# Ends of the last two layers worked by halves of the tokens: one half projected while the other goes through residual and norms

## The chip, the cores and the metric

The kernel runs on one core of a Trainium2 chip. The core has five engines with a queue of instructions each: TensorE (PE in the profile; PEld is its weight load) multiplies matrices, VectorE (DVE), ScalarE (ACT) and GpSimd (POOL) work element by element, SyncE (SP) issues the DMAs. An engine takes the instructions of its queue in order and waits at each until what it needs is there. The metric is the time of one launch on the device in microseconds; the median of three runs before the change is 2830.22 us (2822.88, 2830.22 and 2830.51).

## The reference, cut to what matters

Two blocks of two layers each work on x, 512 tokens of 1024 features, in float32. The last layer of the second block is the one that matters here (`l` is 1, `need_ctx` false):

```python
y, yc = mixer_odd(h, hc, rows, cols, od_w_in[o], od_qk_norm[o], od_lambda[o], od_subln[o],
                  od_w_out[o], diff_lambda_init(l), need_ctx)      # ends in concat(oc, od) @ w_out
x = x + g1 * rms_norm_2(y, norm_g[l, 1])
h = rms_norm_2(x, norm_g[l, 2]) * (1.0 + sc2) + sh2
x = x + g2 * rms_norm_2(swiglu(h, ffn_w_in[l], ffn_w_out[l]), norm_g[l, 3])

def swiglu(h, w_in, w_out):
    g, u = jnp.split(h @ w_in, 2, axis=-1)
    return (jax.nn.silu(g) * u) @ w_out                            # hidden width 2816
```

There are two ends: the mixer's output projection, then residual, norm and the norm ahead of the feed-forward part; and the second feed-forward projection, then norm, residual and the output. Every norm needs the sum of squares over all 1024 features of a token; tokens are independent of each other.

## The kernel before, in words

Activations lie with features on the 128 partitions: x is a tile of 128 x 8 x 512 (feature within a block, block `k`, token). A float32 product is made of three matmuls on halves of the mantissa: `hi` and `lo` of the weights (`wh`, `wl`) with `hi` and `lo` of the activations (`hh`, `hl`; `hid` for the hidden layer). `dense` makes one unit, 128 output features for all tokens, from one call of `weights`: SP loads `wr` (three buffers, L417), ScalarE casts it to `wh` (L422), and POOL subtracts to get `wl` (L398), except that every third unit's goes to VectorE (L400); `wh` and `wl` have two buffers each. A buffer `wr` is free once `wl` is made.

A projection (`out_proj`, and the last loop of `ffn`) runs over eight units `f`. For each, `proj` adds the matmul's result into y (VectorE, L625), squares it (ScalarE, L503) and sums the squares (POOL, L631). Units go in turn to the PSUM tags `d` and `b`, two buffers each.

`boundary` then works all 512 tokens at once. `rstd` sums the squares over partitions by small matmuls against a column of ones, scales them (VectorE, L481), takes the power -1/2 (POOL, L483) and spreads the result by transposing matmuls (L498). `postnorm_tile` makes the residual in eight tiles, a product on VectorE (L576) and a sum (L577) by turns on POOL and VectorE. `prenorm_steps` squares x, sums in seven VectorE additions (L515, L518), calls `rstd` again, and `norm_tile` makes `hh` and `hl` tile by tile (L554 to L560). Where `early` holds weights, `outer` then runs the first four units of the feed-forward part, with the loop over `k` outside, so that it can start with the first norm tile; `prepare` loads and splits those four weights (`u0` to `u3`) during the projection.

The mixer's output projection runs in two parts: inputs 0 to 3 are projected earlier (`out_head`), and the part in question has inputs 4 to 7, so its weights are 128 x 512 and a unit has 12 matmuls. The feed-forward part works its 22 hidden blocks in groups of 8, 8 and 6, each group projected and added into y; the last one has units of 128 x 768 and 18 matmuls.

The order of the work on each engine is set by a scheduler that takes the recorded instructions by their priority. `weave` interleaves streams of steps by rate: (stream, rate, offset of priority).

Of the kernel before, what the change touches and what calls it, by code (L numbers as in the profile page):

```python
# [11 lines left out]
F32 = mybir.dt.float32  # L12
F32R = mybir.dt.float32r
# [10 lines left out]
KD = D // 128  # L24
S = 512
# [174 lines left out]
class Net:  # L200
# [136 lines left out]
    def first(self, g, n):  # L337
        for _ in range(n):
            next(g)
            yield  # L340
# [196 lines left out]
            except StopIteration as e:  # L537
                return e.value

    def prenorm_steps(self, x, T, gain, shift, pool=None, al=None):  # L540
# [4 lines left out]
        h = self.new_h(T, pool)  # L545
        for k in range(n):
            self.norm_tile(h, x, k, T, r, gain, shift, al)
            yield
        return h
# [56 lines left out]
            yield  # L606
            return h, dict(enumerate(acc))

    def outer(self, ws, h, acc, ks=range(KD)):

        for k in ks:
            w = slice(k * 128, k * 128 + 128)
            for (hi, lo), a in zip(ws, acc):
                self.mm(a, hi[:, w], h[0][:, k, :], k == 0, False)
                self.mm(a, hi[:, w], h[1][:, k, :], False, False)
                self.mm(a, lo[:, w], h[0][:, k, :], False, k == KD - 1)

    def proj(self, f, ps, y, sq, T, first=True, last=True):

# [1111 lines left out]

        return self.lagged((block(h) for h in range(4)), -50)

    def ffn(self, l, h, T, hid_new, ready={}):
        nc, I = self.nc, self.I
        wi, wo = I["ffn_w_in"], I["ffn_w_out"]
        y, sq = self.oy(T), None
        for gi, (j0, n) in enumerate(HGROUPS):
            hid = hid_new()
            for j in range(n):  # L1740
                pg, pu = (ready.pop(2 * (j0 + j) + i) if ready else
                          self.dense(wi[l, i * NFH + j0 + j].rearrange("p k c -> p (k c)"), h, T, tag="db"[i])
                          for i in range(2))
                g = self.silu2(pg, T)
                nc.vector.scalar_tensor_tensor(g, g, 0.5, pu, op0=ALU.mult, op1=ALU.mult)  # L1745
                self.split(g, hid[0][:, j, :], hid[1][:, j, :], 1.0, "dve" if j in ([0, 2, 4, 6], [7])[l] else "pool")
                yield
            for f in range(KD):
# [21 lines left out]
    def run(self):  # L1770
# [125 lines left out]
        with self.phase("early") as ph:  # L1896
            early = []

            def prepare():
                for u in range(4):  # L1900
                    src = I["ffn_w_in"][1, u % 2 * NFH + u // 2].rearrange("p k c -> p (k c)")
                    early.append(self.weights(src, 1024, (ph, f"u{u}")))
                    yield

            y, sq = self.weave((self.out_proj(I["od_w_out"], h, S, y, range(4)), 8, 0),
                               (prepare(), 4.2, 0))
            h, ready = self.weave((self.boundary(y, sq, x4, m(1), m(2), x1, early), 1, 0))
            self.close_y()
            self.stage(low=3)
            with self.phase("ffn") as ph:  # L1910
                hid = lambda: [self.tl(ph, [128, KD, S], F32R, "hid", 2) for _ in range(2)]
                y, sq = self.result(self.ffn(1, h, S, hid, ready))
        self.result(self.boundary(y, sq, x1, m(3), None, self.out))

# [66 lines left out]
```

## Time and profile before

| | us |
|---|---|
| runs, median of three | 2830.22 |
| the profiled execution, its own time | 2819.89 |
| its span, first to last instruction | 2818.1 |
| TensorE busy | 2455.0 (87%) |
| VectorE, ScalarE, POOL busy | 1258.7, 1188.2, 1079.4 (45%, 42%, 38%) |

The profiled execution is 10.3 us below the median of the runs. Times in rows are microseconds from the start of its span, so the span ends at 2818.1. In a row of the timeline the bracket at the end is how long the engine was idle before, and what ended the wait. TensorE's matmuls are pipelined: a row's duration overlaps the next one, so the pace is read from the starts.

### The profile page before, as it was taken

To read this page: it belongs to the slowest core of one execution; us is meant where nothing else is said; L and a number is where in the kernel's file an instruction comes from. 1 tells how busy PE (TensorE), PEld (TensorE's weight loads), DVE (VectorE), ACT (ScalarE), POOL (GpSimd) and SP (SyncE) were. 2 spreads that over 40 slices of the span, in tenths; PEclk is the share of its full clock that TensorE was granted. 3 is DMA by queue.
4 is the path that set the end of the run, shared out by engine and by line. 5 is a ranking of instruction groups with operands and counts; after the bars stand their busy time and mean duration, and the time that the engine had idled before them with its cause. 6 is when DMAs were issued, how large, how long until landed. Compare 5 with 4: busy or idle time off the path is not lost. (4 is left out here: it accounts for less than half of the span.)

```text
span 2818.1 us, 35394 instructions
## 1 busy us (share of the span) xinstructions
PE 2455.0 (87%) x13052; PEld 1994.9 (71%) x13052; DVE 1258.7 (45%) x2065; ACT 1188.2 (42%) x2227; POOL 1079.4 (38%) x754
## 2 busy tenths in 40 slices
PE   6988896778888886769999899999888989799997
PEld 4765666666666665648998777777776777688886
DVE  3655357235646644445442631212645767421212
ACT  3534365333547534445554522222434646332222
POOL 2435235344533551213455732322542222443334
PEclk9988998888979987879999999999988989899998
DMA  7364644344344652335553545454444253333332
GB/s 244 121 205 156 207 165 154 107 140 162 104 124 139 213 182 100 116 112 143 174 159 135 186 135 172 149 169 133 148 140 158 90 153 113 113 100 97 94 97 75
DMA packets 170816, 400.56 MB, mean 142 GB/s; under 512 B 19378, under 2 KB 60820, under 8 KB 167316
## 3 DMA queue, kind: packets, MB, share of 16 engines
q1 hardware_dynamic: 170644, 398.31, 43.7%
q8 instruction: 103, 1.69, 0.2%
q14 instruction: 69, 0.57, 0.1%
HBM read 339.85 MB, written 58.39 MB: 141 GB/s over the span
## 5 line engine op out<-in xcount | busy, mean ns | idle before, releaser
L398 POOL TENSOR_TENSOR wl<-wr,wh 128x1024 fp32r<-128x1024 f32 (+3 forms) x245 | 538.2, 2198 | 899.5 <-ACT wh L422 451.5
L422 ACT CAST wh<-wr 128x1024 fp32r<-128x1024 f32 (+3 forms) x367 | 353.8, 964 | 706.5 <-PE d L389 279.5
L389 PE MATMUL d<-hh,wh 128*128 128x512 f32 x960 | 398.4, 415 | 19.7 <-ACT hh L556 7.8
L389 PE MATMUL d<-hl,wh 128*128 128x512 f32 x960 | 394.0, 410 | 1.9 <-DVE hl L557 0.9
L389 PE MATMUL d<-hh,wl 128*128 128x512 f32 x960 | 263.5, 403 | 0.0
L400 DVE SCALAR_TENSOR_TENSOR wl<-wr,wh 128x1024 fp32r<-128x1024 f32 (+3 forms) x122 | 152.1, 1246 | 227.8 <-PE d L389 91.9
L389 PEld LDWEIGHTS d<-hh,wh 128*128 128x128 f32 x960 | 190.6, 199 | 62.2 <-ACT hh L556 8.4
L389 PEld LDWEIGHTS d<-hl,wh 128*128 128x128 f32 x960 | 189.7, 198 | 42.5 <-issue 2.5
L389 PEld LDWEIGHTS d<-hh,wl 128*128 128x128 f32 x960 | 185.0, 195 | 39.6 <-issue 1.6
L400 DVE SCALAR_TENSOR_TENSOR pg<-b,pg 128x512 fp32r<-128x512 f32 (+1 forms) x208 | 137.2, 665 | 68.7 <-ACT pg L404 67.2
L389 PE MATMUL b<-hh,wh 128*128 128x512 f32 x416 | 164.2, 395 | 0.0
L389 PE MATMUL b<-hl,wh 128*128 128x512 f32 x416 | 163.2, 392 | 0.0
L934 POOL TENSOR_TENSOR oy<-pg,pg 64x256 f32<-64x256 f32 (+1 forms) x72 | 57.7, 802 | 262.3 <-DVE pg L932 91.3
L404 ACT CAST pg<-b 128x512 fp32r<-128x512 f32 (+1 forms) x208 | 117.1, 570 | 80.2 <-PE b L909 68.2
L882 DVE TENSOR_REDUCE sm<-s 128x1 f32<-128x768 f32 (+3 forms) x144 | 120.7, 846 | 26.6 <-PE s L389 25.9
L389 PE MATMUL d<-hc,wh 128*128 128x256 f32 x656 | 105.4, 311 | 23.7 <-DVE rp L400 11.8
L950 DVE SCALAR_TENSOR_TENSOR rp<-rp,d 128x512 f32<-128x512 f32 (+1 forms) x77 | 46.7, 607 | 165.5 <-ACT rp L949 165.4
L1745 DVE SCALAR_TENSOR_TENSOR rp<-rp,b 128x512 f32<-128x512 f32 (+1 forms) x64 | 38.1, 595 | 175.3 <-PE b L389 174.8
L389 PE MATMUL d<-hid,wh 128*128 128x512 f32 (+1 forms) x528 | 114.7, 361 | 1.5 <-POOL hid L398 1.5
L389 PEld LDWEIGHTS d<-hc,wh 128*128 128x128 f32 x656 | 94.9, 211 | 28.3 <-ACT wh L422 12.2
L389 PE MATMUL b<-hid,wh 128*128 128x512 f32 (+1 forms) x528 | 110.8, 361 | 0.0
L389 PE MATMUL b<-hh,wl 128*128 128x512 f32 x416 | 103.8, 389 | 0.0
(416 smaller groups left out, 5143.2 us busy)
## 6 DMA issues: line engine op xcount, KB each, us to landing
wr<-in_ffn_w_in SPq DMA_DIRECT2D x132, 512.0 KB
mr<-in_ada_w SPq DMA_DIRECT2D x96, 512.0 KB
wr<-in_ffn_w_out SPq DMA_DIRECT2D x48, 512.0 KB
x<-x SPq DMA_DIRECT2D x20, 1024.0 KB
wr<-in_w_in SPq DMA_DIRECT2D x38, 512.0 KB
mr<-in_w_mod SPq DMA_DIRECT2D x32, 512.0 KB
wr<-in_ev_w_in SPq DMA_DIRECT2D x20, 512.0 KB
wr<-in_ffn_w_out SPq DMA_DIRECT2D x24, 384.0 KB
```

The costliest lines, as they stand in the source:

```text
L389: self.nc.tensor.matmul(out, lhsT, rhs, start=start, stop=stop)
L398: self.nc.gpsimd.tensor_sub(out, src, hi)
L400: self.nc.vector.scalar_tensor_tensor(out, src, scale, hi, op0=ALU.mult, op1=ALU.subtract)
L404: self.nc.scalar.copy(hi, src)
L422: nc.scalar.copy(hi[:, :n], raw[:, :n])
L882: nc.vector.reduce_max(c, s, axis=AX.X, negate=True)
L934: nc.gpsimd.tensor_tensor(d, sel(t), sel(rs), op=ALU.mult)
L950: nc.vector.scalar_tensor_tensor(t, t, 1.0, ps, op0=ALU.add, op1=ALU.mult)
L1745: nc.vector.scalar_tensor_tensor(g, g, 0.5, pu, op0=ALU.mult, op1=ALU.mult)
```

## The change

`ending` takes the place of `out_proj` with `boundary` at the last layer's first end, and of the last group's loop with `boundary` at its second. `proj_half` projects the eight units for one half of the tokens (256 columns), loading and splitting each unit's weights for each half. First half 0 is projected, with `prepare` beside it; then half 1, woven with `norm(0)`: residual, store of x and norm of half 0. Then `norm(1)` is woven with `first(0)`, the early matmuls of half 0, and `first(1)` follows. At the second end there is no early part, and `norm(1)` comes last. `prenorm_steps` can write into a given tile, `outer` can start and stop a sum at other places, and `ffn` can return ahead of its last projection. Tiles `bp` for the residual are ten of half the width, not eight of the full one.

```diff
+    def proj_half(self, c, wsrc, h, y, ks):
+
+        cols, sq = self.half(c), None
+        hv, yv = [t[:, :, cols] for t in h], [t[:, :, cols] for t in y]
+        for f in range(KD):
+            ps = self.dense(wsrc(f), hv, S // 2, ks, "db"[f % 2])
+            sq = self.proj(f, ps, yv, sq, S // 2, False)
+            yield
+        return sq
+
+    def ending(self, proj, y, xsrc, gain, nxt, xdst, early=(), beside=None):
...
+            al = partial(self.tl, ph, dt=F32, tag="bp", bufs=10), self.bank
+            h = self.new_h(S) if nxt is not None else None
+            acc = []
+
+            def norm(c, sq):
+                cols = self.half(c)
+                xv = x[:, :, cols]
+                yield from self.postnorm_steps(xv, [t[:, :, cols] for t in y], sq, S // 2, gain, al)
+                for i in range(2):
+                    nc.sync.dma_start(xdst[:, 4 * i:4 * i + 4, cols], xv[:, 4 * i:4 * i + 4])
+                if nxt is not None:
+                    yield from self.prenorm_steps(xv, S // 2, *nxt, al=al, into=[t[:, :, cols] for t in h])
+
+            def first(c):
+                cols = self.half(c)
+                for k in range(KD):
+                    self.outer(early, [t[:, :, cols] for t in h], [a[:, cols] for a in acc], [k], c == 0, c == 1)
+                    yield
+
+            sq = self.weave(*[(proj(0), 8, 0)] + [(beside, 8, 0)] * (beside is not None))
+            sq = self.weave((proj(1), 8, 0), (norm(0, sq), 17, 0))
+            if not early:
+                self.steps(norm(1, sq))
+                return h
...
+            self.weave((norm(1, sq), 17, 0), (first(0), 8, -150))
+            self.steps(first(1))
+            return h, dict(enumerate(acc))
...
-            y, sq = self.weave((self.out_proj(I["od_w_out"], h, S, y, range(4)), 8, 0),
-                               (prepare(), 4.2, 0))
-            h, ready = self.weave((self.boundary(y, sq, x4, m(1), m(2), x1, early), 1, 0))
...
+            wsrc = lambda f: I["od_w_out"][f, :, 4:8].rearrange("p k c -> p (k c)")
+            ho, yo = h, y
+            h, ready = self.ending(lambda c: self.proj_half(c, wsrc, ho, yo, range(4, 8)), y, x4, m(1), m(2), x1, early,
+                                   prepare())
...
+            f = self.ffn(1, h, S, hid, ready, True)
...
+            self.ending(lambda c: self.proj_half(c, wsrc, hidden, y, range(n)), y, x1, m(3), None, self.out)
```

On POOL, at the first end. Before, from a late unit's low part to the power of the sums (`sm_20985`); `wl` is a unit's low part, `rp` the sum of squares:

```order
L398 TENSOR_TENSOR wl_20893<-wr_20890,wh_20892 128x512
L631 TENSOR_TENSOR rp_20778<-rp_20778,rp_20858 128x512
L398 TENSOR_TENSOR wl_20922<-wr_20919,wh_20921 128x512
L631 TENSOR_TENSOR rp_20778<-rp_20778,rp_20887 128x512
L398 TENSOR_TENSOR wl_20945<-wr_20942,wh_20944 128x512
L631 TENSOR_TENSOR rp_20778<-rp_20778,rp_20910 128x512
L631 TENSOR_TENSOR rp_20778<-rp_20778,rp_20939 128x512
L398 TENSOR_TENSOR wl_21247<-wr_21244,wh_21246 128x1024
L483 TENSOR_TENSOR sm_20985<-sm_20983,mhalf 128x4
```

Now, from the fourth early weight's low part (`u3l`) to the power for half 0 (`sm_21005`):

```order
L398 TENSOR_TENSOR u3l_20882<-wr_20879,u3h_20881 128x1024
L398 TENSOR_TENSOR wl_20888<-wr_20885,wh_20887 128x512
L686 TENSOR_TENSOR rp_20790<-rp_20790,rp_20905 128x256
L398 TENSOR_TENSOR wl_20934<-wr_20931,wh_20933 128x512
L686 TENSOR_TENSOR rp_20790<-rp_20790,rp_20928 128x256
L398 TENSOR_TENSOR wl_20957<-wr_20954,wh_20956 128x512
L686 TENSOR_TENSOR rp_20790<-rp_20790,rp_20951 128x256
L398 TENSOR_TENSOR wl_21022<-wr_21019,wh_21021 128x512
L398 TENSOR_TENSOR wl_21051<-wr_21048,wh_21050 128x512
L483 TENSOR_TENSOR sm_21005<-sm_21003,mhalf 128x2
```

An early weight's low part has come to POOL, ahead of half 0's fifth unit (`wl_20888`), and two low parts of half 1 (`wl_21022`, `wl_21051`) stand ahead of half 0's power.

On TensorE, at the second power of half 0 at the first end (`b_21128` takes its ones-matmuls, `b_21135` its transposes, `b_21180` is unit 5 of half 1, `d_21212` unit 6):

```order
L389 MATMUL b_21128<-blk,bp_21105 128x1 x2
L389 MATMUL d_21212<-hh_19715,wh_21208 128x256
L389 MATMUL d_21212<-hl_19716,wh_21208 128x256
L389 MATMUL d_21212<-hh_19715,wh_21208 128x256
L389 MATMUL d_21212<-hl_19716,wh_21208 128x256
L389 MATMUL d_21212<-hh_19715,wl_21209 128x256 x2
L498 MATMUL b_21135<-ident,sm_21133 128x128 x2
L389 MATMUL b_21180<-hh_19715,wh_21176 128x256
```

Before, nothing was left to project there:

```order
L389 MATMUL b_20974<-blk,rp_20778 128x1 x4
L389 MATMUL b_20974<-blk,rp_20962 128x1 x4
L498 MATMUL b_20987<-ident,sm_20985 128x128 x4
L389 MATMUL b_21041<-blk,bp_21018 128x1 x4
L498 MATMUL b_21050<-ident,sm_21048 128x128 x4
L389 MATMUL d_21093<-hh_21055,u0h_20782 128x512
```

Units 5 and 7 of half 1 have moved behind the transposes of half 0's second norm.

On SP, at the end of the program, before:

```order
L417 DMA wr_23204<-in_ffn_w_out 128x768 [waits DMAHW0_49,DVE_49]
L417 DMA wr_23233<-in_ffn_w_out 128x768 [waits DMAHW1_49,Pool_49]
L417 DMA wr_23262<-in_ffn_w_out 128x768 [waits DMAHW2_49,Pool_49]
L417 DMA wr_23291<-in_ffn_w_out 128x768 [waits DMAHW3_49,DVE_49]
L593 DMA out<-x_23326 128x2048 [waits DVE_49,Pool_49] x2
```

Now:

```order
L417 DMA wr_23885<-in_ffn_w_out 128x768 [waits DMAHW3_49,Pool_49]
L649 DMA out<-x_23470 128x4x256 [waits DVE_49,Pool_49]
L417 DMA wr_23914<-in_ffn_w_out 128x768 [waits DMAHW5_49,Activation_49,Pool_49]
L649 DMA out<-x_23470 128x4x256 [waits DVE_49,Pool_49]
L417 DMA wr_23943<-in_ffn_w_out 128x768 [waits DMAHW4_49]
L649 DMA out<-x_23470 128x4x256 [waits DVE_49,Pool_49] x2
```

The two stores of half 0 stand ahead of the loads of the last two units of half 1.

## Rows read from the trace of the kernel before

**Rows 1.** Busy time by stretches; columns: stretch, length, busy (count) per engine, clock, DMA.
```profile
2393.40:2413.30 19.90, 18.96 (x84) 15.34 (x83) 10.03 (x11) 11.41 (x18) 16.86 (x13) 1.00 0.55 166
2413.30:2436.20 22.90, 5.90 (x33) 4.97 (x33) 14.37 (x24) 5.84 (x11) 10.44 (x7) 0.58 0.37 138
2436.20:2460.90 24.70, 24.70 (x97) 19.72 (x98) 8.77 (x12) 7.71 (x12) 5.21 (x4) 0.91 0.00 1
2766.30:2799.80 33.50, 33.24 (x145) 26.97 (x144) 8.13 (x11) 10.06 (x14) 16.34 (x11) 1.00 0.16 47
2799.80:2818.10 18.30, 3.14 (x21) 2.54 (x19) 8.99 (x14) 0.63 (x1) 7.23 (x5) 0.57 0.28 115
```

**Rows 2.** Timeline, first end; columns: start, us, engine, line, operation, out<-in, count, idle before.
```profile
2413.18 2.35 POOL L398 TENSOR_TENSOR wl<-wr,wh 128x1024 fp32r<-128x1024 f32 x1
...
2415.50 1.02 POOL L483 TENSOR_TENSOR sm<-sm,mhalf 128x4 f32<-128x4 f32 x1
...
2417.60 2.06 DVE L576 SCALAR_TENSOR_TENSOR bp<-oy,x,b 128x512 f32<-128x512 f32 x3 [2.17 <-PE b L498]
...
2424.79 0.98 DVE L577 TENSOR_TENSOR x<-x,bp 128x512 f32<-128x512 f32 x1
...
2429.42 0.69 DVE L518 TENSOR_TENSOR bp<-bp,bp 128x512 f32<-128x512 f32 x1
...
2436.16 0.79 PE L389 MATMUL d<-hh,u0h 128*128 128x512 f32 x1 [1.60 <-ACT hh L556]
```

**Rows 3.** Timeline of TensorE, 256-column matmuls of the context's feed-forward part.
```profile
1564.16 1.98 PE L389 MATMUL b<-hc,wh 128*128 128x256 f32 x16
1565.97 1.07 PE L389 MATMUL b<-hc,wl 128*128 128x256 f32 x8
```

**Rows 4.** Timeline, the first end's projection: POOL, ScalarE, VectorE and the loads.
```profile
2395.29 2.55 POOL L398 TENSOR_TENSOR wl<-wr,wh 128x512 fp32r<-128x512 f32 x2 [5.86 <-PE b L389]
...
2396.61 0.80 SPq L417 DMA_DIRECT2D wr<-in_od_w_out  x2
...
2397.79 1.29 POOL L631 TENSOR_TENSOR rp<-rp,rp 128x512 f32<-128x512 f32 x1
...
2397.86 0.33 SPq L417 DMA_DIRECT2D wr<-in_ffn_w_in  x1
...
2399.28 0.62 ACT L422 CAST wh<-wr 128x512 fp32r<-128x512 f32 x1 [1.86 <-DMA wr<-in_od_w_out]
...
2402.15 1.05 ACT L422 CAST u3h<-wr 128x1024 fp32r<-128x1024 f32 x1 [0.89 <-DMA wr<-in_ffn_w_in]
...
2403.24 1.62 DVE L400 SCALAR_TENSOR_TENSOR u3l<-wr,u3h 128x1024 fp32r<-128x1024 f32 x1 [1.05 <-ACT u3h L422]
...
2403.88 2.13 POOL L631 TENSOR_TENSOR rp<-rp,rp 128x512 f32<-128x512 f32 x1
```

**Rows 5.** Groups by line and shape, whole run; busy and mean ns of one, then idle before.
```profile
L398 POOL TENSOR_TENSOR wl<-wr,wh 128x768 fp32r<-128x768 f32 x26 | 49.6, 1907 | 48.1 <-ACT wh L422 26.3 <-PE d L389 14.4 <-issue 5.1
L625 DVE TENSOR_TENSOR oc<-d,oc 128x256 f32<-128x256 f32 x8 | 3.4, 423 | 7.2 <-PE d L389 7.1
L503 ACT ACTIVATE rp<-oc 128x256 f32<-128x256 f32 x16 | 6.6, 414 | 3.3 <-DVE oc L625 2.9
```

**Rows 6.** Timeline of POOL, a sum of squares of 256 columns, undisturbed.
```profile
1596.25 0.74 POOL L631 TENSOR_TENSOR rp<-rp,rp 128x256 f32<-128x256 f32 x1
```

**Rows 7.** Timeline, the second end.
```profile
2798.45 1.53 PE L389 MATMUL b<-hid,wl 128*128 128x512 f32 x6
2799.83 0.94 PE L389 MATMUL s<-blk,rp 128*128 128x1 f32 x8
...
2804.99 2.07 DVE L576 SCALAR_TENSOR_TENSOR bp<-oy,x,s 128x512 f32<-128x512 f32 x3 [2.31 <-PE s L498]
...
2809.65 3.94 SPq L593 DMA_DIRECT2D out<-x  x2
...
2812.18 0.98 DVE L577 TENSOR_TENSOR x<-x,bp 128x512 f32<-128x512 f32 x1
```

More of the change, by code (lines that the diff above doesn't have):

```diff
@@ L538, in run_through, with prenorm_steps @@
                 return e.value
-    def prenorm_steps(self, x, T, gain, shift, pool=None, al=None):
+    def prenorm_steps(self, x, T, gain, shift, pool=None, al=None, into=None):
         nc = self.nc
@@ L544, in prenorm_steps @@
         r = self.rstd(self.square_sums([x[:, k, :] for k in range(n)], T, al), T, al=al)
[L545 removed]
+        h = into or self.new_h(T, pool)
         for k in range(n):
@@ L607, in boundary, with outer @@
             return h, dict(enumerate(acc))
-    def outer(self, ws, h, acc, ks=range(KD)):
+    def outer(self, ws, h, acc, ks=range(KD), first=True, last=True):
         for k in ks:
@@ L613, in outer, with half @@
             for (hi, lo), a in zip(ws, acc):
-                self.mm(a, hi[:, w], h[0][:, k, :], k == 0, False)
+                self.mm(a, hi[:, w], h[0][:, k, :], first and k == 0, False)
                 self.mm(a, hi[:, w], h[1][:, k, :], False, False)
-                self.mm(a, lo[:, w], h[0][:, k, :], False, k == KD - 1)
+                self.mm(a, lo[:, w], h[0][:, k, :], False, last and k == KD - 1)
+    def half(self, c):
+        return slice(c * S // 2, (c + 1) * S // 2)
+    def proj_half(self, c, wsrc, h, y, ks):
[6 more added lines that the diff above has]
+        return sq
@@ L1747, in ffn @@
                 yield
+            if open_end and gi == len(HGROUPS) - 1:
+                return y, hid, (j0, n)
             for f in range(KD):
@@ L1903, in prepare @@
                     yield
-            y, sq = self.weave((self.out_proj(I["od_w_out"], h, S, y, range(4)), 8, 0),
-                               (prepare(), 4.2, 0))
-            h, ready = self.weave((self.boundary(y, sq, x4, m(1), m(2), x1, early), 1, 0))
[L1908 to L1913, printed above, removed]
+            wsrc = lambda f: I["od_w_out"][f, :, 4:8].rearrange("p k c -> p (k c)")
+            ho, yo = h, y
+            h, ready = self.ending(lambda c: self.proj_half(c, wsrc, ho, yo, range(4, 8)), y, x4, m(1), m(2), x1, early,
+                                   prepare())
+        self.close_y()
+        self.stage(low=3)
+        with self.phase("ffn") as ph:
+            hid = lambda: [self.tl(ph, [128, KD, S], F32R, "hid", 2) for _ in range(2)]
+            f = self.ffn(1, h, S, hid, ready, True)
+            self.result(self.first(f, 38))
+            box = {}
+            self.steps(self.keep(box, f))
+            y, hidden, (j0, n) = box["result"]
+            wsrc = lambda f: I["ffn_w_out"][1, f, :, j0:j0 + n].rearrange("p k c -> p (k c)")
+            self.ending(lambda c: self.proj_half(c, wsrc, hidden, y, range(n)), y, x1, m(3), None, self.out)
 def _layout(a):
```

12 lines of the change are left out of this document (11 added, 1 removed).

## The prediction

> **What bounds the kernel now.** I read four views in this order: the busy table of the page (TensorE busy 87% of the span, every other engine under half), the slices under it, then the busy time by stretches of the two layer ends, then the instructions of those ends in order of time. The stretches [rows 1] are where the reader should look. While the output projection runs (2393.4 to 2413.3) TensorE is busy 18.96 of 19.9 us. Then it is idle: of the next 22.9 us it works 5.90, at a granted clock of 0.58 (a mean between its levels of 1.2 and 2.4 GHz). Then it works without a gap through the "early" matmuls of the next layer (24.70 of 24.70 us). The last projection (33.24 of 33.5 us) and the tail behind it (3.14 of 18.3 us) show the same at the very end. So two stretches, 22.9 and 18.3 us, 41.2 in all, are residual and norms on which TensorE waits. They are all that the change can win.
>
> The instructions [rows 2] say what ends last in the first of them. POOL takes the square root of the sums at 2415.50, VectorE works the eight residual tiles from 2417.60 to 2425.77 (12 instructions, 8.2 us), then seven sums of squares to 2430.11 (the last at 2429.42), a second root and the norm tiles; the first early matmul starts at 2436.16. This is one chain from engine to engine, about 20.7 us from root to matmul. At the end of the program the same chain is shorter by the second norm [rows 7]: last projection matmuls done at 2799.83, VectorE starts at 2804.99, ends at 2813.16, and the second store (issued right then, behind the first of 2809.65) ends the span at 2818.10, 4.94 us later.
>
> **What a half costs.** A 256-column matmul is no dearer per column: sixteen of them stand from 1564.16 to 1565.97, 113 ns each [rows 3]; of 512 columns six stand from 2798.45 to 2799.83, 230 ns each [rows 7]. So splitting costs TensorE itself nothing. The other engines pay a fixed part twice. VectorE needs 0.42 us for 128x256 where 128x512 took 0.69, POOL's sums 0.74 where 1.29, ScalarE's squares 0.41 [rows 2, 4, 5, 6].
>
> What is truly doubled is the weights: each half loads each unit, casts it on ScalarE and takes its low part on POOL (two of three) or VectorE. A unit of the first end is 128x512: 1.28 us on POOL [rows 4]; of the second 128x768: 1.91 mean [rows 5]. Per unit the first end has only 12 matmuls x 113 ns = 1.36 us of TensorE. POOL has 2/3 x 1.28 + 0.74 = 1.59 us. So **in the first end POOL, no longer TensorE, sets the pace**; in the second, TensorE's 18 x 113 = 2.03 us stands against POOL's 2/3 x 1.91 + 0.74 = 2.01, nearly even.
>
> **First end, step by step.** I follow POOL's queue as the order now stands, from 2393.8 (last split of the layer's input done, as before). Up to the root of the first half it has two low parts of 1024 columns (2.35 us each [rows 2]), six of 512 and six sums: 4.7 + 7.7 + 4.4 = 16.8 us, so 2410.6 at the earliest. But it waits for loads. A buffer is free when its low part is done; from a load of 256 KB to its cast are 2.7 us (2396.61 to 2399.28), of 512 KB behind others 4.3 (2397.86 to 2402.15) [rows 4], and there are three buffers. The fourth early weight now stands ahead of units 4 to 7 in POOL's queue: its buffer is free at 2396.2, it is cast at 2400.5, its low part runs 2401.5 to 2403.9. The two low parts of the second half that the queue puts ahead of the root come from loads issued at 2408.5 and 2410.6; with 2.7 and the cast of 0.62 the second starts at 2413.9 and ends at 2415.2. So the first half's root is taken at about 2415.2, bounds 2410.6 and 2418. Before, the root of all tokens was taken at 2415.50. **The first half gains no head start**, and five units of the second are still to be projected.
>
> From there to the first early matmul was 20.7 us. For a half: 12 residual instructions at 0.40 pitch 4.8 (before 8.2), seven sums 2.8 (4.3), the two roots with their matmuls about 1.5 less, so 20.7 - 3.4 - 1.5 - 1.5 = 14.3. Between them VectorE does, for the second half, five sums into y and two low parts, 5 x 0.42 + 2 x 0.8 (half of 1.62 [rows 4]) = 3.7; ScalarE puts casts and squares ahead of the first norm tile (one 1024 cast 1.05 and four of 0.4), 2.6. Sum 20.6: first early matmul at about 2436, where it was. The second half's last units lie inside this, because TensorE's queue puts the second root's transposes ahead of units 5 and 7; they end at about 2433.
>
> The early matmuls of the first half (96 x 113 ns = 10.9 us, to 2447) lie beside the second half's residual. That starts once POOL has the last sum and ScalarE the last square, root at about 2439.5. Then 1.6 to the first residual instruction, 4.8 + 1.2 (a 1024 low part in between, 1.62 where it was stretched) + 2.8 + 0.4 on VectorE, 3.3 for the second root, 0.8 to the matmul: 2439.5 + 14.9 = 2454.4, less up to 2 if squares run closely behind: I take 2453. TensorE waits from 2447 to then. Its 96 matmuls of the second half take 10.9 us at the full clock; before, the first ones after the idle stretch ran at the lower level (the stretch at 0.91 took 24.70 us for 96 x 0.233 = 22.4 [rows 1]), so 2 us more: end at 2465. Before it was 2460.9. Term: **+4 us**, bounds -17 (POOL hides all, see the gain) and +12.
>
> The cover of the first half's matmuls is the second half's residual; were it gone they would cost 10.9 us.
>
> **Second end.** Loads and low parts keep up with TensorE for the first half: 16 units x 2.06 from the old start, less what lay under the wait for the last hidden tile, make TensorE 1.2 us later. At the first half's root the same queueing occurs: TensorE's queue has the transposes after seven matmuls of unit 2 and ahead of unit 1, and POOL takes the root after unit 2's low part, 1.91 us. I count a stall of 2.0. SP's queue now has the store of the first half's tiles ahead of the last two loads. The store waits for the fourth residual tile, some 4 us after the root; behind it stand a load (2.7), a cast (between 0.62 and 1.05) and a low part (1.91). Unit 6 and 7 then come about 2 us late. Nothing else waits on SP there. So projection +5.2 (bounds +1 and +9). The tail: the statistics piece of 5.16 us (2799.83 to 2804.99) loses 0.27 + 0.22 on VectorE and ScalarE and about 1.5 on half the small matmuls and root, to 3.2; 8.2 becomes 4.8; the last store is 512 KB in place of 1 MB that followed another, 4.94 becomes 3.9 (halving 2.3 us of moving; its pieces are shorter, 1 KB in place of 8, so bounds 3.2 and 4.9). 11.9 for 18.3: -6.4. Term: **-1 us**, bounds -6 and +4.
>
> **Two engines beside each other.** POOL's adds of 128x512 show 2.13 us beside VectorE's low part stretched to 1.62, where two in a row without it took 2.55 [rows 4]: 0.84 more each. Fifteen VectorE instructions with two inputs in SBUF lie on each half's chain (four residual adds, seven sums, four low parts of norm tiles), and POOL is busy beside the first half's. I let two or three of them meet a POOL one: +2 for the first end, bounds 0 and +12.6 (all fifteen). The Trainium skill, page "SBUF — State Buffer", section "SBUF: two separate sides", says that a VectorE instruction with two SBUF inputs and a POOL one exclude each other for the whole instruction; that would make every meeting dear, as in the slower rival below. By that rule, the trace agrees in the pair shown (2.13 and 1.62).
>
> **The sum.** 4 - 1 + 2 = +5 us on the profiled execution of 2819.89 (span 2818.1): 2825. The runs before have a median of 2830.22, 10.3 above it, so I forecast 2830 + 5 = **2835**, 0.2% more. What this kernel's measurement can tell from no change is about 0.3%, 8.5 us.
>
> **Rivals.** *Gain.* The halves stream at TensorE's pace and POOL keeps up: the second projection ends at 2393.4 + 16 x 1.36 = 2415.2, its chain of about 15 us brings the first matmul of the second half to 2431, the end to 2444, 17 less; the second end -5. At full size 2808; with half of the queueing 2819. For it: POOL's 16.8 us would allow the first root five us earlier. Against: the three buffers and the 2.7 us of a load, which hold whatever POOL does. *Slower, the lock.* On the first half's chain each of the 15 instructions with two SBUF inputs waits for a POOL one: up to 0.84 each (2.13 less 1.29), 12.6, and I reckon half, 6, and as much on POOL's own queue, which the late projection then pays: +12 to +15, so 2844. It decides if POOL is busy over some 80% from 2417 to 2436. For it: POOL was busy 16.86 of 19.9 us before with half the units [rows 1]. Against: sums from PSUM into y and gains from PSUM did not stretch. *Nothing hidden.* If the first half's matmuls start only when the second half is ready (a root behind a load), their 10.9 us come back: 2846; it shares the slower side.
>
> **How the numbers follow.** The forecast 0.50 (own range 2826 to 2848: 0.34 of it within 0.3%, 0.13 slower, 0.03 faster), the gain 0.20 (0.17 faster, 0.03 within), the two slower ones 0.25 (0.22 slower, 0.03 within), and 0.05 that both ends cancel otherwise, within. Faster 0.20, within 0.45, slower 0.35. The range for eight in ten reaches from the milder gains, 2815, to the slower rivals, 2850.
>
> **What would show it.** In the profile after: first root of the half-wide kind about where the full one was (2415), not before 2411; TensorE's gaps in 2396 to 2433 ended by POOL's or ScalarE's weights; early matmuls of 256 columns from about 2436 with a gap of some 6 us between the two halves, next layer's dense matmuls from 2465; the tail from last projection matmul to the end near 12 us. I am wrong if the projection's 16 units run at 1.4 us each, or if the first half's early matmuls start before 2428.

## The result and the profile after

The changed kernel takes 2840.35 us (median of 17 runs, 2830.86 to 2847.32), the kernel before 2822.88 in 17 runs beside them: a ratio of 1.0053, 95% interval 1.0039 to 1.0067. That is 0.53% slower, some 15 us (the means are 15.0 us apart; the medians alone, 17.5).

The two profiled executions are 22.4 us apart (spans 2840.5 and 2818.1). Part of it stands ahead of the change: the low part of the first early weight, which both kernels issue at the same place, starts at 2384.82 before and at 2391.43 after.

```profile
2384.82 2.36 POOL L398 TENSOR_TENSOR u0l<-wr,u0h 128x1024 fp32r<-128x1024 f32 x1 [4.71 <-ACT u0h L422]
```

These 6.6 us say nothing of the change: in the profiles of the twelve variants below, that start lies anywhere from 2379.9 to 2389.2, and the changed kernel's is the latest by 2.2. So all stages are measured from points inside one trace. The first end is taken from this low part to the first dense matmul behind the early ones (2460.91 before), the second end from the first matmul of the last projection to the end of the span (2766.30 to 2818.1 before).

| stage, us | before | after | difference |
|---|---|---|---|
| first end | 76.1 | 88.0 | +11.9 |
| FFN between the ends | 305.4 | 305.7 | +0.3 |
| second end | 51.8 | 55.4 | +3.6 |

They add up to 15.8, close to the 15 us of the ratio. The busy times of the changed kernel by stretches, columns as in [rows 1]: the projection of the first half, of the second half, the gap, the early matmuls of the first half, the second gap, those of the second half, then the last projection and the tail.

```profile
2399.30:2421.10 21.80, 16.33 (x98) 15.14 (x98) 8.97 (x12) 9.53 (x18) 16.34 (x13) 0.77 0.38 131
2421.10:2445.40 24.30, 16.71 (x102) 15.20 (x100) 17.14 (x37) 11.34 (x25) 14.60 (x16) 0.79 0.42 138
2445.40:2449.10 3.70, 0.44 (x5) 0.42 (x4) 3.64 (x6) 3.64 (x10) 3.62 (x4) 1.00 0.65 208
2449.10:2462.70 13.60, 13.60 (x103) 13.13 (x102) 9.11 (x21) 4.07 (x10) 6.78 (x9) 0.87 0.21 71
2462.70:2466.50 3.80, 1.23 (x7) 0.82 (x7) 1.69 (x6) 0.52 (x2) 0.71 (x1) 1.00 0.64 238
2466.50:2479.40 12.90, 12.86 (x97) 12.76 (x98) 4.04 (x11) 4.99 (x12) 3.25 (x4) 0.87 0.44 164
2785.10:2829.10 44.00, 39.07 (x303) 37.44 (x301) 18.02 (x35) 18.24 (x30) 33.68 (x28) 0.96 0.44 132
2829.10:2840.50 11.40, 1.04 (x6) 0.71 (x6) 4.89 (x14) 0.42 (x1) 3.95 (x5) 0.66 0.27 92
```

The idle 22.9 us of before [rows 1] have gone: no stretch of the first end leaves TensorE idle for more than 4 us. But the projection, 19.9 us before, now takes 46.1 in two halves, and TensorE is neither full in it (33.04 busy) nor at its higher clock (0.77 and 0.79). The idle time was not removed; it was spread between the units. The instructions of the changed kernel's first end, in order of time:

```profile
2391.43 2.35 POOL L398 TENSOR_TENSOR u0l<-wr,u0h 128x1024 fp32r<-128x1024 f32 x1 [4.74 <-ACT u0h L422]
...
2408.57 0.38 PE L389 MATMUL d<-hh,wh 128*128 128x256 f32 x1 [2.42 <-ACT wh L422]
...
2412.18 1.22 PE L389 MATMUL d<-hh,wl 128*128 128x256 f32 x4 [2.25 <-POOL wl L398]
...
2422.34 1.27 POOL L398 TENSOR_TENSOR wl<-wr,wh 128x512 fp32r<-128x512 f32 x1 [0.95 <-ACT wh L422]
2423.57 0.71 POOL L483 TENSOR_TENSOR sm<-sm,mhalf 128x2 f32<-128x2 f32 x1
...
2431.35 1.82 DVE L515 TENSOR_TENSOR bp<-bp,bp 128x256 f32<-128x256 f32 x2
2432.61 0.51 PE L389 MATMUL d<-hh,wl 128*128 128x256 f32 x2 [3.58 <-POOL wl L398]
...
2434.03 2.84 DVE L515 TENSOR_TENSOR bp<-bp,bp 128x256 f32<-128x256 f32 x4
...
2435.86 0.58 PE L389 MATMUL d<-hh,wh 128*128 128x256 f32 x1 [1.78 <-ACT wh L422]
...
2439.95 0.63 PE L498 MATMUL b<-ident,sm 128*128 128x128 f32 x2
2440.23 0.56 PE L389 MATMUL b<-hh,wh 128*128 128x256 f32 x1
...
2444.79 0.64 PE L389 MATMUL b<-hh,wl 128*128 128x256 f32 x4
...
2445.46 0.51 ACT L556 ACTIVATE hh<-bp,ada 128x256 fp32r<-128x256 f32 x1 [0.21 <-PE b L389]
...
2448.69 0.61 PE L389 MATMUL b<-blk,rp 128*128 128x1 f32 x4 [3.26 <-POOL rp L686]
2449.15 0.36 PE L389 MATMUL d<-hh,u0h 128*128 128x256 f32 x1
...
2453.21 0.71 POOL L483 TENSOR_TENSOR sm<-sm,mhalf 128x2 f32<-128x2 f32 x1 [2.12 <-DVE sm L481]
...
2466.54 0.39 PE L389 MATMUL d<-hh,u0h 128*128 128x256 f32 x1 [1.11 <-ACT hh L556]
...
2479.45 0.40 PE L389 MATMUL b<-hl,wh 128*128 128x512 f32 x1
```

TensorE's gaps inside the projection are ended by ScalarE's high parts and POOL's low parts (2.42, 2.25, 3.58, 1.78 us). POOL takes the first half's root right behind a low part. The second half's last matmuls end at 2445.43, and ScalarE's first hh of the first half follows 0.03 us later. The second half's root, at 2453.21, is 29.6 us behind the first half's.

### The profile page after: what moved, and what is told of

Its sections match the earlier page's. It is cut to its first block, busy times and chain, and to the rows that moved or that the text cites. A ratio compares the mean times of both kernels' runs of the same rounds, so it can differ in the third digit from the quotient of the medians.

```text
span 2840.5 us, 36317 instructions
## 1 busy us (share of the span) xinstructions
PE 2467.9 (87%) x13388; PEld 2019.5 (71%) x13388; DVE 1273.3 (45%) x2132; ACT 1204.9 (42%) x2279; POOL 1107.5 (39%) x792
## 5 line engine op out<-in xcount | busy, mean ns | idle before, releaser
L398 POOL TENSOR_TENSOR wl<-wr,wh 128x1024 fp32r<-128x1024 f32 (+3 forms) x254 | 554.3, 2183 | 890.1 <-ACT wh L422 422.5
L422 ACT CAST wh<-wr 128x1024 fp32r<-128x1024 f32 (+3 forms) x383 | 365.1, 954 | 725.6 <-PE d L389 283.2
L389 PE MATMUL d<-hh,wh 128*128 128x512 f32 (+1 forms) x976 | 401.7, 412 | 25.1 <-ACT wh L422 11.0
L389 PE MATMUL d<-hl,wh 128*128 128x512 f32 (+1 forms) x976 | 397.2, 408 | 3.3 <-POOL hl L398 1.4
L389 PE MATMUL d<-hh,wl 128*128 128x512 f32 (+1 forms) x976 | 263.7, 398 | 6.2 <-POOL wl L398 6.2
L400 DVE SCALAR_TENSOR_TENSOR wl<-wr,wh 128x1024 fp32r<-128x1024 f32 (+3 forms) x129 | 159.8, 1238 | 239.5 <-PE d L389 103.1
L389 PEld LDWEIGHTS d<-hh,wl 128*128 128x128 f32 x976 | 186.0, 194 | 45.4 <-POOL wl L398 6.9
L389 PE MATMUL b<-hh,wh 128*128 128x512 f32 (+1 forms) x432 | 167.8, 390 | 0.2 <-DVE y L680 0.2
L389 PE MATMUL b<-hl,wh 128*128 128x512 f32 (+1 forms) x432 | 166.5, 387 | 0.0
L400 DVE SCALAR_TENSOR_TENSOR pg<-b,pg 128x512 fp32r<-128x512 f32 (+1 forms) x208 | 137.4, 666 | 64.3 <-ACT pg L404 63.0
L989 POOL TENSOR_TENSOR oy<-pg,pg 64x256 f32<-64x256 f32 (+1 forms) x72 | 57.7, 802 | 263.4 <-DVE pg L987 73.6
L389 PE MATMUL b<-hh,wl 128*128 128x512 f32 (+1 forms) x432 | 106.1, 385 | 0.4 <-POOL wl L398 0.4
```

Source lines behind the costliest of these rows:

```text
L389: self.nc.tensor.matmul(out, lhsT, rhs, start=start, stop=stop)
L398: self.nc.gpsimd.tensor_sub(out, src, hi)
L400: self.nc.vector.scalar_tensor_tensor(out, src, scale, hi, op0=ALU.mult, op1=ALU.subtract)
L422: nc.scalar.copy(hi[:, :n], raw[:, :n])
L989: nc.gpsimd.tensor_tensor(d, sel(t), sel(rs), op=ALU.mult)
```

## The experiments

One table of what was measured. The first end and the second end are read from each profile as above, the ratio is to the kernel before, with its 95% interval. The three columns in the middle are points of the first end, in us from the same low part: the first early matmul, the end of the second half's last projection matmul, and the second half's root (the third power on POOL).

| kernel | ratio | first early matmul | projection of half 1 ends | root of half 1 | first end, us | second end, us |
|---|---|---|---|---|---|---|
| before | 1 | 51.3 | | | 76.1 | 51.8 |
| changed | 1.0053 (1.0039 to 1.0067) | 57.7 | 54.0 | 61.8 | 88.0 | 55.4 |
| first_only | 1.0052 (1.0033 to 1.0071) | 57.9 | 54.2 | 62.1 | 88.4 | 53.0 |
| second_only | 0.9987 (0.9973 to 1.0002) | 51.6 | | | 76.2 | 50.6 |
| root_ahead | 1.0073 (1.0055 to 1.0091) | 53.0 | 52.4 | 62.2 | 88.0 | 63.8 |
| shared6 | 1.0022 (1.0008 to 1.0036) | 52.9 | 52.2 | 58.4 | 82.7 | 48.9 |
| reuse_h | 1.0065 (1.0047 to 1.0083) | 52.2 | 54.6 | 62.6 | 89.0 | 55.0 |
| banks | 1.0052 (1.0032 to 1.0073) | 53.9 | 53.3 | 61.2 | 88.5 | 56.8 |
| shared6_h | 1.0003 (0.9989 to 1.0017) | 49.3 | 53.0 | 57.1 | 81.7 | 48.8 |
| shared6_h_late | 1.0009 (0.9994 to 1.0024) | 53.6 | 53.8 | 58.1 | 82.7 | 49.1 |
| shared6_h_banks | 1.0000 (0.9981 to 1.0018) | 50.2 | 40.5 | 54.0 | 79.2 | 49.0 |
| second_shared6 | 1.0003 (0.9990 to 1.0017) | 51.4 | | | 76.1 | 49.7 |
| pe_sums | 1.0056 (1.0034 to 1.0077) | 57.3 | 56.7 | 64.3 | 90.3 | 54.1 |
| all_pe_sums | 1.0011 (0.9992 to 1.0029) | 45.4 | 44.3 | 53.9 | 80.6 | 48.7 |

In every kernel with halves at the first end, the end comes 24.3 to 27.3 us after the second half's root; it follows neither the first early matmul nor the end of the projection. The same code repeats within 0.4 us at the first end (76.1, 76.2 and 76.1; 88.0 and 88.4), but at the second end the old code of before took 51.8 and, in first_only, 53.0, so there a difference of about 1 us says nothing.

**Which end?** The kernel first_only has the changed kernel's first end and the old second one, second_only the other way round. Their edits to the changed kernel, first_only above and second_only below:

```
-            f = self.ffn(1, h, S, hid, ready, True)
...
-            self.ending(lambda c: self.proj_half(c, wsrc, hidden, y, range(n)), y, x1, m(3), None, self.out)
+            y, sq = self.result(self.ffn(1, h, S, hid, ready))
+        self.result(self.boundary(y, sq, x1, m(3), None, self.out))
```

```
-            h, ready = self.ending(lambda c: self.proj_half(c, wsrc, ho, yo, range(4, 8)), y, x4, m(1), m(2), x1, early,
-                                   prepare())
+            y, sq = self.weave((self.out_proj(I["od_w_out"], h, S, y, range(4)), 8, 0),
+                               (prepare(), 4.2, 0))
+            h, ready = self.weave((self.boundary(y, sq, x4, m(1), m(2), x1, early), 1, 0))
```

> Halves at the mixer's end only; the last FFN group and the end of the program as before the change. Theory (the cost is made where the halves are worked, and most of it at the first end): the stretch from TensorE's first half-wide projection to the next layer's dense matmuls is 9 to 11 us longer than before, the rest as before, so 2832 to 2834 us against 2823, 0.35% slower. Rival A (the time is lost between the ends, by another layout or another order of the loads): the first end shows less than 4 us and the FFN between the ends 5 or more. Rival B (the first end costs nothing by itself): no change within 0.2%.

> Halves at the end of the program only; the mixer's end as before the change. Theory: the last projection takes 44 us where it took 33.5, the tail behind it 12 where it took 18.3, so +3 to +4 us: 2826, 0.1% slower, and with the other end alone it adds up to the +15 us of both. Rival (a gain that the first end hides): faster by 4 to 6 us, since the tail is 6.5 us shorter and the projection would be as long as before once the loads are not disturbed by the end before.

The first end alone has the whole cost, as the theory said (2837 us, a little more than expected). The second end alone is no cost, against its theory of 3 to 4 us more; its interval just reaches 1, so a gain of 0.1% is not shown either, and the rival's 4 us faster is not excluded. The numbers of the two do not add up to the 3.6 us that the second end cost in the changed kernel: the same lines took 50.6 us in second_only and 55.4 in the changed kernel. The traces show one difference. In the changed kernel the low part that stands ahead of the first half's root is POOL's:

```profile
2806.26 1.83 POOL L398 TENSOR_TENSOR wl<-wr,wh 128x768 fp32r<-128x768 f32 x1 [0.20 <-ACT wh L422]
2808.05 0.71 POOL L483 TENSOR_TENSOR sm<-sm,mhalf 128x2 f32<-128x2 f32 x1
...
2808.81 0.69 PE L498 MATMUL b<-ident,sm 128*128 128x128 f32 x2 [1.21 <-POOL sm L483]
2809.15 2.91 PE L389 MATMUL b<-hid,wh 128*128 128x256 f32 x12
```

In second_only the same place has VectorE's turn, and POOL is free for the root:

```profile
2786.83 0.71 POOL L483 TENSOR_TENSOR sm<-sm,mhalf 128x2 f32<-128x2 f32 x1
...
2787.07 0.96 DVE L400 SCALAR_TENSOR_TENSOR wl<-wr,wh 128x768 fp32r<-128x768 f32 x1 [0.32 <-DVE sm L481]
...
2787.59 0.43 PE L498 MATMUL b<-ident,sm 128*128 128x128 f32 x2 [0.22 <-POOL sm L483]
2787.78 1.66 PE L389 MATMUL b<-hid,wh 128*128 128x256 f32 x12
```

VectorE takes every third low part in turn (`flip`), and the first end's eight more loads shift that turn by two. So an edit at one end decides which engine stands in the way 300 us later. That this accounts for all of the 4.8 us was not tested.

**The queue of POOL.** The root of the first half put ahead:

```
-            sq = self.weave((proj(1), 8, 0), (norm(0, sq), 17, 0))
+            sq = self.weave((proj(1), 8, 0), (norm(0, sq), 17, 200))
```

> All as in the changed kernel, but everything of the first half's residual and norms is put 200 places earlier in the order, so that on POOL the first half's root goes ahead of the second of the two low parts (wl) that stood before it. Theory (POOL's queue holds the root up): the wait of TensorE for the root at the second end, 1.2 us, and the slower clock behind it, some 2 us, go; the first end wins the 1.3 us of a low part at the first half, of which the second half's chain shows little: 2 to 4 us less than the changed kernel, 2837. Rival (what sets the end is the second half's projection, which now stands behind more residual work): as the changed kernel or up to 4 us slower.

The theory was wrong: no gain at the first end, though the first early matmul came 4.7 us earlier there, and in the profile the second end is 8.4 us longer. The ratio's interval still overlaps that of the changed kernel, so the rival's "up to 4 us slower" is not excluded. The places in the order are shared by all engines: TensorE's ones-matmuls of the norm moved into the first half's last unit and waited there for POOL's sums, and those of the second half waited for them again.

```profile
2795.09 0.99 PE L389 MATMUL b<-blk,rp 128*128 128x1 f32 x4 [2.49 <-POOL rp L686]
...
2800.41 0.71 POOL L483 TENSOR_TENSOR sm<-sm,mhalf 128x2 f32<-128x2 f32 x1 [0.87 <-DVE sm L481]
...
2826.04 1.87 PE L389 MATMUL b<-blk,rp 128*128 128x1 f32 x8 [4.17 <-POOL rp L686]
```

With the last projection's start at 2774.58 the root came 25.8 us after it; in the changed kernel it came 22.9 after (2808.05 less 2785.12).

**The weights.** Six of eight units split once for both halves:

```
+        for i, f in enumerate(order if c else range(KD)):
+            if c == 0:
+                kept[f] = self.weights(wsrc(f), len(ks) * 128, (ph, f"s{f}") if f in keep else None)
+            ws = kept[f] if f in keep or f >= 6 and i < 2 else None
+            ps = self.dense(wsrc(f), hv, S // 2, ks, "db"[i % 2], ws if c else kept[f])
```

> All as in the changed kernel, but six of the eight units' weights are split once for both halves: units 0 to 3 stay in buffers of their own, units 7 and 6 are still in theirs when the second half begins, which goes in the order 7, 6, 0, 1, 2, 3, 4, 5. Only units 4 and 5 are loaded and split a second time. Theory (the doubled loads, casts and low parts are what the halves cost): the second half's projection runs at TensorE's pace, 1.4 us a unit at the first end and 2.1 at the second; the next layer's dense matmuls come 16 to 20 us earlier than in the changed kernel, the end of the program 5 to 8 more; 2812 to 2820 us, faster than before the change by 0.1 to 0.4%. Rival (the chain of residual and norms, worked twice on VectorE and ScalarE, sets the end whatever the weights do): within 4 us of the changed kernel, 2836 to 2842.

In between and outside both expectations: 2826.1 us, 0.31% below the changed kernel (1.0022 against 1.0053). The first end won back 5.3 of its 11.9 us, the second end 6.5. So at the first end the doubled weights are near half of the cost: loads, casts and low parts, and with the low parts also what POOL does beside VectorE; the edit removes them together and changes the order of the units. The 6.5 us of the second end are not all theirs: second_only, which loads and splits everything twice, took 50.6 us there, and second_shared6 49.7.

**One tile, two PSUM buffers.** Two more things tie the halves together. The norm's output `h` shares its buffer with the projection's input; and the norms' small PSUM tiles (ones-sums, spread root) take turns with every second unit of the second half in two buffers. The first was undone by writing into the old tile (reuse_h), the second by wide PSUM buffers for the first half's norms (banks):

```
-            h = self.new_h(S) if nxt is not None else None
...
-                                   prepare())
+                                   prepare(), ho)
```

```
-                xv = x[:, :, cols]
+                xv, al = x[:, :, cols], (bp, self.bank if c else self.flat)
```

> All as in the changed kernel, but the norm at the first end writes its halves into the tile that the projection reads, and not into a new tile that shares its buffer; so the first half's norm tiles wait only for the first half's projection. Theory (beside the weights, the one buffer of hh and hl keeps the halves apart: in the changed kernel ScalarE's first hh of the first half began 0.03 us after the last matmul of the second half's projection): the first early matmuls come 2 to 4 us earlier, more of them lie beside the second half's projection, and the next layer starts 2 to 4 us earlier; 2833 to 2836 us, 0.35 to 0.5% over before. Rival (the weights and VectorE hold both halves; the buffer only happened to come free then): as the changed kernel, 2837 to 2840.

> All as in the changed kernel, but the small sums and the spread root of the first half's norms go into PSUM buffers of the wide kind (s), and not into the two buffers (b) that every second unit of the second half is projected into. Theory (the second half's units 5 and 7 stand behind the first half's second root because they take its buffers: in the changed kernel unit 5 began 2440.23, behind the transposes of 2439.95): TensorE projects unit 5 and 6 ahead of the second root, the second half's projection ends some 2 us earlier and so does the first end; but units 4 to 7 still wait for loads and low parts, so no more: 2833 to 2837, 0.35 to 0.5% over before. Rival (loads and low parts pace the second half alone): as the changed kernel, 0.53% over before or more.

Neither gains by itself (1.0065 and 1.0052). In banks the theory's step did happen, unit 5 and most of unit 6 went ahead of the second root's transposes, but the second half's projection ended only 0.7 us earlier (53.3 for 54.0). In reuse_h the step happened too: the first early matmul came 52.2 us after the early weight's low part (2439.64 less 2387.4), 5.5 earlier than in the changed kernel. But the second half did not come earlier:

```profile
2439.64 0.34 PE L389 MATMUL d<-hh,u0h 128*128 128x256 f32 x1
...
2446.57 1.01 PE L389 MATMUL b<-blk,rp 128*128 128x1 f32 x4 [2.40 <-POOL rp L685]
```

Its ones-matmuls start 59.1 us after that low part, in the changed kernel 57.3. The first half's early matmuls were covered already; the second half sets the end.

With the weights out of the way, both were tried again, and the order of the norm too: shared6_h is shared6 with the edit of reuse_h, shared6_h_late has the line below besides, shared6_h_banks has the edit of banks in its place.

```
-            sq = self.weave((proj(1), 8, 0), (norm(0, sq), 17, 0))
+            sq = self.weave((proj(1), 8, 0), (norm(0, sq), 17, -60 if early else 0))
```

> Six units' weights split once for both halves, and the norm written into the projection's tile. Theory: in the kernel with shared weights alone the first half's norm tiles stood ready from 2428 and hh was written from 2432.2, behind the last projection, which itself stood behind the second root's transposes in TensorE's queue; without that wait the first early matmul comes 4 us earlier and the next layer starts 3 to 6 us earlier: 2820 to 2823, equal to before within 0.15%. Rival (the second half's residual sets the end, and the first half's early matmuls were hidden anyway): as shared weights alone, 2826.

> As the kernel before it, with the first half's residual and norms put 60 places later in the order at the first end, so that on TensorE two more units of the second half go ahead of its transposes. Theory (TensorE's 6 us of waiting for the second root with units still to project behind it are part of the cost): another 1 to 3 us off the second half, 2818 to 2821. Rival (the second half waits on VectorE, which the projection's sums then hold): the same as, or up to 3 us slower than, the kernel before it.

> Six units' weights split once, the norm written into the projection's tile, and the first half's norms in PSUM buffers of their own. Theory (three things kept the second half behind the first: weights twice, one tile for hh and hl, two PSUM buffers for units and norms; with all three gone TensorE projects all of the second half while VectorE works the first half's residual): the second half's root comes 5 to 8 us earlier than with the first two alone, the next layer starts 4 to 7 us earlier; 2815 to 2818, 0.1 to 0.25% faster than before, and no slower than halves at the end of the program alone. Rival (VectorE, which has the residual and norms of both halves one after the other, is the bound then): within 2 us of the kernel without the buffers, 2820 to 2822.

Without the tile's wait the first end is 1.0 us shorter in the profile; the ratio falls from 1.0022 to 1.0003, some 5 us, but the two intervals overlap. The later order is worth nothing. The buffers took another 2.5 us off the first end in the profile; the ratio, 1.0000, can't tell it from 1.0003. In this kernel TensorE has all of the second half projected before the first half's second root, as wanted, and the first end is still 3.1 us longer than before. VectorE is where it waits. Its sums of squares, six for the first half, then six for the second:

```profile
2427.26 6.07 DVE L515 TENSOR_TENSOR bp<-bp,bp 128x256 f32<-128x256 f32 x6
...
2434.14 0.72 PE L389 MATMUL s<-blk,bp 128*128 128x1 f32 x4 [4.48 <-DVE bp L518]
...
2450.90 2.09 DVE L515 TENSOR_TENSOR bp<-bp,bp 128x256 f32<-128x256 f32 x6
```

The same six instructions take 6.07 us while POOL adds squares and makes a low part, and 2.09 while POOL is idle:

```profile
2427.57 0.92 POOL L688 TENSOR_TENSOR rp<-rp,rp 128x256 f32<-128x256 f32 x1
2428.82 1.75 POOL L688 TENSOR_TENSOR rp<-rp,rp 128x256 f32<-128x256 f32 x2 [0.33 <-ACT rp L503]
2430.53 2.52 POOL L398 TENSOR_TENSOR wl<-wr,wh 128x1024 fp32r<-128x1024 f32 x1
```

**VectorE's sums.** So the sums were given to TensorE, in the changed kernel (pe_sums) and in shared6_h_banks (all_pe_sums): with a plan of eight "n" every square stays in a tile of its own and goes to the ones-matmuls.

```
-        r = self.rstd(self.square_sums([x[:, k, :] for k in range(n)], T, al), T, al=al)
+        r = self.rstd(self.square_sums([x[:, k, :] for k in range(n)], T, al, "n" * 8 if into else "nnvvvvvv"), T, al=al)
```

> All as in the changed kernel, but the eight squares of each half's second norm are added by TensorE (eight pairs of ones-matmuls in place of one pair) and not by seven sums on VectorE. Theory (the second half's chain sets the first end, and the first half's is hidden up to the early matmuls): what counts is the second half's seven sums, 2.5 us in the changed kernel, less some 0.7 for fourteen more small matmuls, so 2 us; the first half's seven, 5.1 us because POOL works beside them, free VectorE for the second half's sums into y, 1 to 2 us more: 2834 to 2836, 0.4% over before. Rival (the loads and low parts of the second half pace everything up to its root): 2 us or less, 0.5% over before.

> The kernel with six units' weights split once, one tile for hh and hl and PSUM buffers of their own, and the squares added by TensorE. There the first half's six sums took 6.07 us beside POOL where the second half's took 2.09. Theory (VectorE's chain with POOL beside it is what is left of the cost): the first half's second root comes 4 to 6 us earlier, the second half's residual can start that much earlier, its own sums are 2 us less: the first end 4 to 7 us shorter, below the one of the kernel before the change by 1 to 4; with the second end 2814 to 2818, 0.15 to 0.3% faster than before. Rival (the second half's root is bound by its projection): 2 us less, 2820, no change from before.

No gain in either (1.0056 and 1.0011), against the theory. In all_pe_sums the first half did get ahead: its second root came 3.3 us earlier than in shared6_h_banks (42.63 for 45.95 us after the early weight's low part), its first early matmul 4.9. But the second half's root stayed where it was (53.9 for 54.0). The matmuls of the second half's last unit ended at 2430.41; their sum into y then stood in VectorE's queue behind the first half's norm tiles, one of which took 2.32 us beside a low part on POOL, where one with POOL idle took 0.48:

```profile
2429.70 0.71 PE L389 MATMUL b<-hh,wl 128*128 128x256 f32 x4
...
2431.23 2.32 DVE L557 SCALAR_TENSOR_TENSOR hl<-bp,ada,hh 128x256 fp32r<-128x256 f32 x1
...
2435.53 0.41 DVE L682 TENSOR_TENSOR y<-b,y 128x256 f32<-128x256 f32 x1
...
2440.00 0.71 POOL L483 TENSOR_TENSOR sm<-sm,mhalf 128x2 f32<-128x2 f32 x1 [0.55 <-DVE sm L481]
```

Behind that root, VectorE waited for the second half's new ones-matmuls, which stand in TensorE's queue among the early matmuls:

```profile
2450.34 0.16 DVE L481 TENSOR_SCALAR sm<-b 128x2 f32<-128x2 f32 x1 [4.35 <-PE b L389]
```

So the order of the two halves on VectorE still held the second half's root. An order with the second half's sums into y ahead of the first half's norm tiles was not tried.

**A version that beats both?** second_only has the lowest ratio, 0.9987 with an interval that reaches 1.0002. With shared weights besides (second_shared6, the edits of second_only and shared6):

> The first end as before the change; only the end of the program by halves, six of its eight units' weights split once. Theory: the part from the last projection to the end was 51.8 us before, 50.6 with halves alone and 48.9 with shared weights, so 3 to 6 us less than before: 2816 to 2819, 0.1 to 0.2% faster. Rival (these few us are the spread of that part, in which the same code took 51.8 and 53.0): no change, 2822.

1.0003: no change. No version here is faster than the kernel before by more than can be measured.

## Why the prediction came out as it did

The time lies in the range (2815 to 2850). The likeliest case, within 0.3% of before, did not happen: 0.53% slower, for which there was a chance of 0.35. I forecast +5 us; the runs show +15. That the time came out only 5 us over the forecast of 2835 is luck in part: the forecast started from the first median of 2830.22, and 17 runs of the same kernel gave 2822.88; 5 us on that are 2828, some 12 below what was measured. The wide range covers the rest.

Step by step, with the changed kernel's times less the 6.6 us by which its trace is late:

| step | forecast | measured |
|---|---|---|
| root of the first half | 2415.2 | 2417.0 |
| first early matmul | 2436 | 2442.5 |
| projection of the second half ends | 2433 | 2438.8 |
| root of the second half | 2439.5 | 2446.6 |
| early matmuls of the second half | 2453 | 2459.9 |
| next layer's dense matmuls | 2465 | 2472.8 |

- "The first half gains no head start": right, and by the queue of POOL as told, 1.8 us off.
- "The second half's last units lie inside this": the step that failed. I took the projection of the last five units as hidden beside the first half's residual, at no cost but 3.7 us of VectorE and 2.6 of ScalarE, and let it end at 2433. It ended 5.8 us later, its root came another 1.3 later, and from the second root on, 26.2 us measured against 25.5 forecast, everything follows. What held the end is the weights first (shared6 wins 5.3 us of the first end back), the tile and the PSUM buffers after that (3.5 together, measured on top of shared6 only). I had seen that TensorE's queue put the transposes ahead of units 5 and 7 and did not ask why; it is the buffers, as banks shows, but with the weights still doubled that is worth 0.7 us. And the end of the projection was the wrong thing to watch: in shared6_h_banks it came 13.5 us earlier than in the changed kernel, the second half's root 7.8 and the end 8.8, since the sums of the second half wait on VectorE for the first half's norm.
- Two slips in the working. Its own terms for the first end give 2453 + 10.9 + 2 = 2465.9 and so +5, not +4. And the row of 2.55 us read as "two in a row" of POOL's adds shows two low parts; the 1.29 us of one add, from which the 0.84 comes, is in the same rows.
- "+2 for the first end" for VectorE beside POOL: too low in size. The first half's seven sums took 5.1 us (1.82, 2.84 and 0.41) where I counted 2.8, and up to 6.07 for six in shared6_h_banks. By the Trainium skill's page "SBUF — State Buffer", section "SBUF: two separate sides", such a pair excludes each other for the whole instruction; the trace agrees (6.07 us beside POOL's 5.19, 2.09 without). That the sums lie on the path that sets the end is not shown: pe_sums and all_pe_sums took them away and won nothing. In all_pe_sums another VectorE instruction, ahead of the second half's sum, was stretched in their place.
- "Slower, the lock" named a time close to the one measured (2844, +12 to +15). Its sign did not come: POOL was to be busy over some 80% from 2417 to 2436, and in those 19 us of the changed kernel, 6.6 later, it was busy 10.93 (58%):

```profile
2423.60:2442.60 19.00, 12.31 (x72) 11.53 (x73) 14.63 (x30) 7.97 (x19) 10.93 (x13) 0.76 0.47 152
```

  So its time is no proof of its cause; it was not tested apart from the weights.
- "Nothing hidden", the rival with the first half's matmuls uncovered, did not happen: they ran from 2449.15 to 2462.7, beside the second half's residual.
- Second end: "-1 us" for the sum of a longer projection (+5.2) and a shorter tail (-6.4). Alone (second_only) it is -1.2, with the projection at 39.2 us for 33.5, but that is no more than the 1.2 us by which the old code differs between two profiles. In the changed kernel the tail is as forecast (12.0 us from the last projection matmul to the end, forecast 11.9), but the projection is 43.4 us, +9.9 and over the upper bound of 9. The stall at the root that I counted at 2.0 was 1.21 us and was followed by matmuls at the lower clock; then TensorE waited for the weights of the last units, 1.29, 0.78 and 0.28 us, and it had waited 1.09 for the last hidden tile:

```profile
2819.03 0.98 PE L389 MATMUL d<-hid,wl 128*128 128x256 f32 x6 [1.29 <-POOL wl L398]
```

## What to carry to other kernels

Before work is split to fill an engine's idle time, list all that the halves will share: weights that are made twice, an output tile in the input's buffer, PSUM buffers that take turns, an engine that is slowed by its neighbour. A half runs beside the other only as far as all of these allow it; undoing one alone can show nothing while another still holds (reuse_h, banks). The time from the second half's last input to its end is what counts, not when the first half starts: three kernels here brought the first early matmul 3.8 to 5.5 us forward and ended no earlier (root_ahead, reuse_h, banks). In the changed kernel the second half still took 21.1 us from its last projection matmul to its first early one (2445.43 to 2466.54), where all tokens together had taken 22.9.

## What was not expected of the hardware

TensorE's granted clock fell behind a wait of 1.21 us. Two stretches of the changed kernel around the second end's root, then the same stretch of second_only, where the wait was 0.22 us; columns as in [rows 1]:

```profile
2805.70:2808.80 3.10, 1.90 (x17) 1.70 (x15) 0.58 (x2) 0.91 (x2) 2.86 (x3) 1.00 0.67 215
2808.80:2812.70 3.90, 3.89 (x20) 3.89 (x21) 2.38 (x6) 0.56 (x1) 2.29 (x3) 0.56 0.36 101
```

```profile
2787.60:2791.50 3.90, 3.90 (x33) 3.90 (x34) 3.74 (x8) 1.70 (x3) 2.66 (x3) 1.00 0.73 203
```

At 0.56 (near its lower level of 1.2 GHz) TensorE did 20 instructions in 3.9 us, at 1.00 (2.4 GHz) 33. Twelve 256-column matmuls took 2.91 us in place of 1.66. By the count, 13 instructions fewer at 0.118 us each, the slow stretch cost about 1.5 us (an estimate from these rows), as much as the stall itself.

But the length of the wait does not decide it. In pe_sums TensorE waited 1.22 us at the same place, and the next 3.9 us ran at 1.00:

```profile
2807.99 0.43 PE L498 MATMUL b<-ident,sm 128*128 128x128 f32 x2 [1.22 <-POOL sm L483]
```

```profile
2808.00:2811.90 3.90, 3.90 (x33) 3.90 (x34) 3.44 (x9) 1.53 (x2) 2.34 (x3) 1.00 0.40 105
```

In reuse_h a wait of 1.48 us there was followed by 1.00 as well, and so was the changed kernel's own wait of 1.29 us at 2819.03. Why the clock fell once and not in these cases is open.
